# A transformer-like block on one core: P7's weights from the kept T2, P2 in P7's stage, late LayerNorm 2 vectors

## The chip, the cores and the metric

The kernel runs on one core of one Trainium2 chip. The metric is the device time of one execution in microseconds, the median over several runs. A second number is the span of the one execution that was profiled: from its first to its last instruction on the chip.

## What is computed

One layer on 512 tokens of width 2048, in float32 with float32 accuracy:

```python
h = layer_norm(x, ln_in_g, ln_in_b)
u = h @ w_in                                   # pool values | q | k | v
m = concat(multi_scale_pool(pool values), stick_breaking_attention(q, k, v)) @ w_out
h = layer_norm(alpha * h + m, ln1_g, ln1_b)
f = relu(h @ w_ff1 + b_ff1) ** 2               # 512 x 8192
f = f @ w_ff2 + b_ff2                          # 8192 x 2048 weights, 64 MiB
out = layer_norm(alpha * h + f, ln2_g, ln2_b)
```

Only the last two lines are touched by the change.

## The kernel before, in words

Each float32 product is made of three passes of the reduced type: an operand is split into a high and a low part, and a helper (`three`, L280) adds high x high, high x low and low x high in one PSUM bank. A weight is loaded (`w2_unit`, L726: 256 rows x 512 columns, 512 KB), its high part is a copy by ScalarE (`th`, L737) and its low part a subtraction by VectorE (`tl`, L738); both by `parts` (L733).

The product with `w_ff2` is done by Winograd's form of Strassen's method, with seven products in place of eight. The inner dimension of 8192 is cut into 16 blocks of 512, four blocks (`PER`) to a slice, so there are four slices (`slice_of`, L757). In each block the left operand is a 2 x 2 of A11, A12, A22 and A21 (tokens in two halves, inner dimension in two halves of 256). Its seven combinations were made earlier and stored to DRAM by POOL (`fh_d`, `fl_d`, L699); `operand` (L716) loads one of them for a whole slice as two tiles of 1 MiB (`oh`, `ol`) on POOL's queue. Four operands have room at a time, so the one asked for fifth takes the buffers of the first. The right operand is a 2 x 2 of b11, b12, b21 and b22 (inner halves, column halves), worked on in columns of 512: n = 0, 1 is the left half, n + 2 the right half. A unit is one product for one (n, u), u being the block in the slice: 12 matmuls. The weights of the products follow a chain kept in SBUF, a tile `c` for each of the eight (n, u):

- stage 1: b11 (P1, operand A11) and T1 = b12 - b11 (P5, operand S1; `c`, L775);
- stage 2: T2 = b22 - T1 (P6, operand S2; `c`, L789) and b22 (P3, operand S4);
- stage 3: b22 - b12 (P7, operand S3; L804), with b22 and b12 loaded again (`b22b`, `b12b`);
- stage 4: b21 (P2, operand A12) and b21 - T2 (P4, operand A22; `c`, L817); in the last slice all of P2, then `norm_out` for token blocks 0 and 1, then P4 for n = 0, then for n = 1 by token blocks, with a `norm_out` after each.

`x` banks collect P1, P6, P7 and P4; `v` banks P5 and P3; `w` banks P2. VectorE adds them to the rows `acc` (L752) after each n.

What sets the order: each engine and each DMA queue works through its instructions in a fixed order. The framework lays that order out when the kernel is built, by priorities and a simulated time line; what stands under `with ahead()` has its priority raised by 400 instructions, so that weights are prepared ahead of the matmuls. How far ahead is bounded by buffers: six `raw` tiles for weights under way (three each in two pools, in turn), four pairs of `th` and `tl`. Weight loads go out on SP's queue, operands on POOL's. At the entry of the slices the `right` pool takes over memory that the stage before held.

`norm_out` (L848) is LayerNorm 2 of 128 tokens: `bn_stats` by VectorE, a short chain of small operations, two operations of 512 columns for each quarter of the row (L859 and L860, with the vectors `ln2g` and `ln2b`) and the store (L861, SP). The first `norm_out` in program order asks for the two vectors (L852, SP, 1 MiB each as spread over 128 partitions), which depend on nothing but the memory of their tiles.

Of the kernel before, what the change touches and what calls it, by code (L numbers as in the profile page):

```python
# [9 lines left out]
F32 = mybir.dt.float32  # L10
F32R = mybir.dt.float32r
AF = mybir.ActivationFunctionType
ALU = mybir.AluOpType

P = 128
N = 512
# [7 lines left out]
def block_kernel(  # L24
# [18 lines left out]
    nc = tc.nc  # L43
# [5 lines left out]
    NQ = D // N  # L49
# [38 lines left out]
    def after(ins, earlier):  # L88

        tc.add_manual_dep(ins.ins, earlier.ins.name, mybir.DependencyInfo(  # L90
            mybir.DependencyClass.Sync, mybir.DependencyReason.DATA), reason="whole bank")
# [188 lines left out]
    def three(bank, a, b, first, last, free=False):  # L280
        (ah, al), (bh, bl) = a, b
        for n, (l, r) in enumerate(((ah, bh), (ah, bl), (al, bh))):
            mm = nc.tensor.matmul(bank, l, r, start=first and n == 0, stop=last and n == 2, skip_group_check=free)  # L283
        return mm
# [246 lines left out]
    for half in range(2):  # L531
        if half:
            v_block(half)
        for pair in (2 * half, 2 * half + 1):
            parts = qk_block(pair)
# [37 lines left out]
    for q in range(NQ - 1):  # L573
        banks = product(cols(w_out2, q * N, order), order, mixh, mixl, [f"o{q}_{tb}" for tb in range(NT)], False,
                        beside_first if q == 0 else
                        lambda i, mm: normed(q, i // 2, i % 2, mm))
# [65 lines left out]
    for t0 in (0, 2 * P):  # L642
        ts_ = slice(t0, t0 + 2 * P)
# [7 lines left out]
    for q in range(NQ):  # L651
        gb = tmp.tile([P, N], F32, tag="w", bufs=3, name=f"g1_{q}")
# [15 lines left out]
    first = pool(ctx, "first", 2, side="right")  # L668
# [4 lines left out]
    PER = 4  # L673
# [34 lines left out]
    right = pool(late, "right", 2)  # L708
# [7 lines left out]
    def operand(s, o):  # L716

        pl = right if turn("op", 2) else first
        both = []
        for d, n in ((fh_d, "h"), (fl_d, "l")):  # L720
            t = pl.tile([P, PER, 2, H2], F32R, tag=f"o{n}", bufs=2, name=f"o{n}{s}_{o}")
            nc.gpsimd.dma_start(f(t), d[s][o].rearrange("p u (i t) -> p u i t", i=2))
            both.append(t)
        return both

    def w2_unit(b, half, q, name):  # L726

        k0 = b * N + half * H2
        raw = (right if turn("raw") else wp).tile([P, 2, N], F32, tag="raw", bufs=3, name=name)
        nc.sync.dma_start(raw, w2[k0:k0 + H2, q * N:(q + 1) * N].rearrange("(c p) n -> p c n", p=P))  # L730
        return raw

    def parts(t, name):  # L733
        pl = right if turn("parts") else wp
        h = pl.tile([P, 2, N], F32R, tag="wh", bufs=2, name=f"th_{name}")
        l = pl.tile([P, 2, N], F32R, tag="wl", bufs=2, name=f"tl_{name}")
        nc.scalar.copy(h, t)  # L737
        nc.vector.tensor_tensor(l, t, f(h), op=ALU.subtract)  # L738
        return h, l

    def times(banks, op, u, w, first, last, ts=(0, 1)):
        (ah, al), (wh, wl) = op, w
        for i in range(2):
            for t in ts:
                ts_ = slice(t * P, (t + 1) * P)
                three(banks[t], (ah[:, u, i, ts_], al[:, u, i, ts_]), (wh[:, i, :], wl[:, i, :]),
                      first and i == 0, last and i == 1, True)

    def accumulate(banks, tb0, q, ts=(0, 1)):
        for t in ts:  # L750
            a = acc[tb0 + t][q]
            nc.vector.tensor_tensor(a, a, banks[t], op=ALU.add)  # L752
# [4 lines left out]
    def slice_of(s):  # L757

        end = s == NS - 1
        ahead = lambda: tc.high_priority(offset=400)  # L760
        units = range(PER)
        x = [pair(f"x{s}_{n}", f"x{n}") for n in range(2)]
        v = [pair(f"v{s}_{n}", f"v{n}") for n in range(2)]
        chain = {}
        with ahead():
            A11, S1 = operand(s, 0), operand(s, 3)
        for n in range(2):
            for u in units:
                b, at, e = s * PER + u, f"{s}_{n}_{u}", (u == 0, u == PER - 1)
                with ahead():  # L770
                    b11 = w2_unit(b, 0, n, f"b11_{at}")
                    b12 = w2_unit(b, 0, n + 2, f"b12_{at}")
                    p1 = parts(b11, f"1_{at}")
                    c = chain[n, u] = right.tile([P, 2, N], F32, tag=f"c{n}{u}", bufs=1, name=f"c_{at}")
                    nc.vector.tensor_tensor(c, b12, b11, op=ALU.subtract)  # L775
                    p5 = parts(c, f"5_{at}")
                times(x[n], A11, u, p1, *e)
                times(v[n], S1, u, p5, *e)
            accumulate(x[n], 0, n)
            accumulate(v[n], 2, n + 2)  # L780
        with ahead():
            S2, S4 = operand(s, 4), operand(s, 6)
        for n in range(2):
            for u in units:
                b, at, e = s * PER + u, f"{s}_{n}_{u}", (False, u == PER - 1)
                with ahead():
                    b22 = w2_unit(b, 1, n + 2, f"b22_{at}")
                    c = chain[n, u]
                    nc.vector.tensor_tensor(c, b22, c, op=ALU.subtract)  # L789
                    p6 = parts(c, f"6_{at}")  # L790
                    p3 = parts(b22, f"3_{at}")
                times(x[n], S2, u, p6, *e)
                times(v[n], S4, u, p3, *e)
            accumulate(x[n], 0, n + 2)
            accumulate(v[n], 0, n + 2)
        with ahead():
            S3 = operand(s, 5)
        for n in range(2):
            for u in units:
                b, at, e = s * PER + u, f"{s}_{n}_{u}", (False, u == PER - 1)  # L800
                with ahead():
                    b22 = w2_unit(b, 1, n + 2, f"b22b_{at}")
                    b12 = w2_unit(b, 0, n + 2, f"b12b_{at}")
                    nc.vector.tensor_tensor(b22, b22, b12, op=ALU.subtract)  # L804
                    p7 = parts(b22, f"7_{at}")
                times(x[n], S3, u, p7, *e)
            accumulate(x[n], 2, n + 2)
        with ahead():
            A12, A22 = operand(s, 1), operand(s, 2)
        w = [pair(f"w{s}_{n}", f"v{n}") for n in range(2)]  # L810

        def second(n, u):
            at = f"{s}_{n}_{u}"
            with ahead():
                b21 = w2_unit(s * PER + u, 1, n, f"b21_{at}")
                c = chain[n, u]
                nc.vector.tensor_tensor(c, b21, c, op=ALU.subtract)  # L817
                p2 = parts(b21, f"2_{at}")
            times(w[n], A12, u, p2, u == 0, u == PER - 1)

        def fourth(n, u):
            with ahead():
                return parts(chain[n, u], f"4_{s}_{n}_{u}")

        for n in range(2):
            for u in units:
                second(n, u)
                if not end:
                    times(x[n], A22, u, fourth(n, u), False, u == PER - 1)
            accumulate(w[n], 0, n)  # L830
            if not end:
                accumulate(x[n], 2, n)
        if end:
            for tb in range(2):
                norm_out(tb)
            for u in units:
                times(x[0], A22, u, fourth(0, u), False, u == PER - 1)
            accumulate(x[0], 2, 0)
            p4 = [fourth(1, u) for u in units]
            for t in range(2):  # L840
                for u in units:
                    times(x[1], A22, u, p4[u], False, u == PER - 1, (t,))
                accumulate(x[1], 2, 1, (t,))
                norm_out(2 + t)

    gb = {}

    def norm_out(tb):  # L848
        if not gb:
            for n, vec in (("g", ln2_g[0]), ("b", ln2_b[0])):  # L850
                t = gb[n] = right.tile([P, NQ, N], F32, tag=f"ln2{n}", bufs=1, name=f"ln2{n}")
                nc.sync.dma_start(t, vec.rearrange("(q n) -> q n", n=N).partition_broadcast(P))  # L852
        st = small.tile([P, NQ, 6], F32, name=f"st2_{tb}", tag="st")
        for q in (2, 3, 0, 1):
            nc.vector.bn_stats(st[:, q, :], acc[tb][q])
        mu, rs = finish_stats(st, f"n2{tb}", const)
        for q in range(NQ):
            a = acc[tb][q]
            nc.vector.scalar_tensor_tensor(a, a, mu, gb["g"][:, q, :], op0=ALU.subtract, op1=ALU.mult)  # L859
            nc.vector.scalar_tensor_tensor(a, a, rs, gb["b"][:, q, :], op0=ALU.mult, op1=ALU.add)  # L860
            nc.sync.dma_start(out2[tb * P:(tb + 1) * P, q * N:(q + 1) * N], a)  # L861
# [36 lines left out]
```

## Time and profile before

| | us |
|---|---|
| median of 3 runs (lowest to highest) | 2025.33 (2020.68 to 2026.61) |
| the profiled execution | 2028.36 |
| its span | 2026.7 |
| TensorE busy (share of the span) | 1940.9 (96%) |
| VectorE busy | 1216.1 (60%) |
| ScalarE busy | 739.4 (36%) |

PE is TensorE, PEld its weight load, DVE VectorE, ACT ScalarE, POOL GpSimd, SP SyncE; L12 is line 12 of the kernel. Times in rows are from the start of the span. A busy PE is not a PE at its peak: matmuls are pipelined, so the number of matmuls in a stretch tells more than the busy time. A wait is put down to what came last by the profile.

### The profile page before, as it was taken

Reading aid. Unit: us, or ns where it says so; the run is one execution under the profiler, and the core shown is the slowest. Engines: PE = TensorE matmul, PEld = TensorE weight load, DVE = VectorE, ACT = ScalarE, POOL = GpSimd, SP = SyncE. Lnnn points to the kernel's source line nnn. Section 1 sums busy time; section 2 is a strip of 40 time slices with the busy share of each in tenths; the row PEclk is TensorE's granted clock in tenths of the full one; section 3 lists DMA queues with packets and bytes.
Section 4 is the critical chain, followed back from the end, with each engine's and each line's share of the span. In section 5 each row is a group of like instructions: output and inputs, shape, how many; then the busy total and the mean of one; then the engine's idle time right before and its main releaser. Section 6 shows DMA issues by size and latency. Waiting matters only on the chain.

```text
span 2026.7 us, 22165 instructions
## 1 busy us (share of the span) xinstructions
PE 1940.9 (96%) x8736; PEld 1595.6 (79%) x8736; DVE 1216.1 (60%) x1513; ACT 739.4 (36%) x898; POOL 115.4 (6%) x162
## 2 busy tenths in 40 slices
PE   6999999999999999999999999969999999999995
PEld 4888888878889888888888888847788778778774
DVE  8445565675469544444344444348677687577788
ACT  3344554651124233333333333324343243333331
POOL 5000000000000000110000010010000000000000
PEclk9999999999999999999999999989999999999998
DMA  5022222225344455755555565567767766587562
GB/s 219 32 93 74 83 84 83 84 89 194 105 137 136 140 166 168 263 206 195 175 166 166 175 206 200 174 252 279 266 224 259 260 212 243 206 295 256 191 224 83
DMA packets 155399, 358.03 MB, mean 177 GB/s; under 512 B 10144, under 2 KB 27680, under 8 KB 147488
## 3 DMA queue, kind: packets, MB, share of 16 engines
q1 hardware_dynamic: 131728, 239.11, 36.2%
q0 software_dynamic: 23424, 117.45, 15.1%
q8 instruction: 68, 1.11, 0.2%
q14 instruction: 35, 0.29, 0.0%
q10 hardware_dynamic: 144, 0.07, 0.0%
HBM read 293.67 MB, written 62.91 MB: 176 GB/s over the span
## 4 chain that ended last, share of the span: by engine, by line
PE 53%; issue 23%; DVE 10%; DMA 10%; POOL 2%; ACT 1%; SPq 0%; DVEq 0%; POOLq 0%; ACTq 0%
PE f L210 9%; PE qk L361 9%; PE x L283 6%; PE o L210 6%; DMA b<-in_w_ff_dram 5%; PE p L210 4%; PE v L283 4%; DVE tl L738 4%; DMA b22b<-in_w_ff_dram 4%; PE o L283 3%; PE w L283 3%; PE f L283 2%; PE v L210 2%; POOL fh_d L699 1%; POOL fl_d L699 1%
## 5 line engine op out<-in xcount | busy, mean ns | idle before, releaser
L210 PE MATMUL f<-h1l,wh_f 128*128 128x512 f32 x960 | 373.8, 389 | 0.0
L210 PE MATMUL f<-h1h,wh_f 128*128 128x512 f32 x960 | 373.8, 389 | 0.0
L210 PE MATMUL f<-h1h,wl_f 128*128 128x512 f32 x960 | 347.1, 389 | 0.0
L184 DVE TENSOR_TENSOR wl_f<-raw_f,wh_f 128x1024 fp32r<-128x1024 f32 x120 | 146.8, 1224 | 276.3 <-ACT wh_f L183 276.3
L183 ACT CAST wh_f<-raw_f 128x1024 fp32r<-128x1024 f32 x120 | 126.4, 1053 | 361.4 <-PE f L210 320.9
L283 PE MATMUL x<-th,oh 128*128 128x512 f32 x512 | 195.8, 397 | 21.2 <-ACT th L737 21.0
L210 PEld LDWEIGHTS f<-h1h,wl_f 128*128 128x128 f32 x960 | 180.3, 188 | 37.4
L210 PEld LDWEIGHTS f<-h1l,wh_f 128*128 128x128 f32 x960 | 180.2, 188 | 37.3
L210 PEld LDWEIGHTS f<-h1h,wh_f 128*128 128x128 f32 x960 | 180.2, 188 | 37.3
L283 PE MATMUL x<-tl,oh 128*128 128x512 f32 x512 | 203.9, 398 | 5.2 <-DVE tl L738 4.8
L283 PE MATMUL x<-th,ol 128*128 128x512 f32 x512 | 202.0, 394 | 0.0
L737 ACT CAST th<-b 128x1024 fp32r<-128x1024 f32 x96 | 100.9, 1052 | 178.9 <-PE v L283 64.6
L737 ACT CAST th<-c 128x1024 fp32r<-128x1024 f32 x96 | 101.1, 1053 | 155.3 <-PE x L283 97.1
L738 DVE TENSOR_TENSOR tl<-b,th 128x1024 fp32r<-128x1024 f32 x96 | 117.0, 1220 | 36.4 <-ACT th L737 36.4
L283 PEld LDWEIGHTS x<-th,oh 128*128 128x128 f32 x512 | 96.1, 189 | 46.4 <-ACT th L737 24.3
L738 DVE TENSOR_TENSOR tl<-c,th 128x1024 fp32r<-128x1024 f32 x96 | 116.9, 1220 | 21.0 <-ACT th L737 20.8
L283 PEld LDWEIGHTS x<-tl,oh 128*128 128x128 f32 x512 | 96.9, 189 | 33.3 <-DVE tl L738 12.0
L283 PEld LDWEIGHTS x<-th,ol 128*128 128x128 f32 x512 | 96.9, 189 | 21.3
L283 PE MATMUL v<-th,oh 128*128 128x512 f32 x256 | 98.9, 398 | 10.5 <-ACT th L737 10.5
L283 PE MATMUL v<-tl,oh 128*128 128x512 f32 x256 | 102.3, 400 | 6.9 <-DVE tl L738 6.9
L283 PE MATMUL v<-th,ol 128*128 128x512 f32 x256 | 101.7, 397 | 0.0
L697 DVE TENSOR_TENSOR fl<-g,fh 128x1792 fp32r<-128x1792 f32 x32 | 64.8, 2025 | 61.4 <-DMA fl_d<-fl 53.8
(212 smaller groups left out, 3453.8 us busy)
## 6 DMA issues: line engine op xcount, KB each, us to landing
b<-in_w_ff_dram SPq DMA_DIRECT2D x128, 512.0 KB, 5.0
raw_f<-in_w_ff_dram SPq DMA_DIRECT2D x120, 512.0 KB, 3.9
fh_d<-fh POOLq DMA_DIRECT2D x32, 896.0 KB, 5.3
fl_d<-fl POOLq DMA_DIRECT2D x32, 896.0 KB, 5.9
oh<-fh_d POOLq DMA_DIRECT2D x28, 1024.0 KB, 7.9
ol<-fl_d POOLq DMA_DIRECT2D x28, 1024.0 KB, 10.6
raw_qk<-in_w_in_dram SPq DMA_DIRECT2D x64, 256.0 KB, 2.9
b22b<-in_w_ff_dram SPq DMA_DIRECT2D x32, 512.0 KB, 6.3
```

The costliest lines, as they stand in the source:

```text
L183: nc.scalar.copy(h, raw)
L184: nc.vector.tensor_tensor(l, raw, f(h), op=ALU.subtract)
L210: mm = nc.tensor.matmul(bank, a, b, start=first and n == 0, stop=last and n == 2)
L283: mm = nc.tensor.matmul(bank, l, r, start=first and n == 0, stop=last and n == 2, skip_group_check=free)
L361: nc.tensor.matmul(bank, a, b, start=kc == 0 and n == 0, stop=kc == KC - 1 and n == 2)
L697: nc.vector.tensor_tensor(l, full, f(h), op=ALU.subtract)
L699: nc.gpsimd.dma_start(d[b // PER][:, :, b % PER, i * H2:(i + 1) * H2].rearrange("o p t -> p o t"), f(t))
L737: nc.scalar.copy(h, t)
L738: nc.vector.tensor_tensor(l, t, f(h), op=ALU.subtract)
```

## The change

In slices 0 to 2, P7's weight b22 - b12 is made as T2 - b11, from the kept `c` and one load of b11. P7 and P2 then alternate in one stage, and `c` becomes b21 - T2 right behind P2's unit; P4 follows as a stage of its own without loads. A22 is asked for after that shared stage in program order. In the last slice P2 comes first, then `norm_out` for token blocks 0 and 1, then P7 (with the same new weight), then P4, for which b21 is loaded a second time, since `c` must stay T2 until P7 is made. The LayerNorm 2 vectors are loaded on POOL's queue, after the last matmul of the last slice's stage 2.

```diff
@@ times
-                three(banks[t], ...)
+                mm = three(banks[t], ...)
+        return mm
@@ slice_of, stage 2
-                times(v[n], S4, u, p3, *e)
+                mm = times(v[n], S4, u, p3, *e)
@@ slice_of, stages 3 and 4
         with ahead():
-            S3 = operand(s, 5)
-        for n in range(2):
-            for u in units:
-                with ahead():
-                    b22 = w2_unit(b, 1, n + 2, f"b22b_{at}")
-                    b12 = w2_unit(b, 0, n + 2, f"b12b_{at}")
-                    nc.vector.tensor_tensor(b22, b22, b12, op=ALU.subtract)
-                    p7 = parts(b22, f"7_{at}")
-                times(x[n], S3, u, p7, *e)
-            accumulate(x[n], 2, n + 2)
-        with ahead():
-            A12, A22 = operand(s, 1), operand(s, 2)
+            S3, A12 = operand(s, 5), operand(s, 1)
         w = [pair(f"w{s}_{n}", f"v{n}") for n in range(2)]
+        def third(n, u):
+            with ahead():
+                b11 = w2_unit(s * PER + u, 0, n, f"b11b_{at}")
+                nc.vector.tensor_tensor(b11, chain[n, u], b11, op=ALU.subtract)
+                p7 = parts(b11, f"7_{at}")
+            times(x[n], S3, u, p7, False, u == PER - 1)
         def second(n, u):
             with ahead():
                 b21 = w2_unit(s * PER + u, 1, n, ...)
-                c = chain[n, u]
-                nc.vector.tensor_tensor(c, b21, c, op=ALU.subtract)
                 p2 = parts(b21, ...)
             times(w[n], A12, u, p2, u == 0, u == PER - 1)
+            return b21
+        def last_of(n, u, b21):
+            with ahead():
+                c = chain[n, u]
+                nc.vector.tensor_tensor(c, b21, c, op=ALU.subtract)
...
+        if not end:
+            for n in range(2):
+                for u in units:
+                    third(n, u)
+                    last_of(n, u, second(n, u))
+                accumulate(x[n], 2, n + 2)
+                accumulate(w[n], 0, n)
+            with ahead():
+                A22 = operand(s, 2)
+            for n in range(2):
+                for u in units:
+                    times(x[n], A22, u, fourth(n, u), False, u == PER - 1)
+                accumulate(x[n], 2, n)
+            return
+        load_vectors(mm)
         for n in range(2):
             for u in units:
                 second(n, u)
-                if not end:
-                    times(x[n], A22, u, fourth(n, u), False, u == PER - 1)
             accumulate(w[n], 0, n)
...
+        with ahead():
+            A22 = operand(s, 2)
+        for tb in range(2):
+            norm_out(tb)
+        for n in range(2):
+            for u in units:
+                third(n, u)
+            accumulate(x[n], 2, n + 2)
+        for u in units:
+            with ahead():
+                last_of(0, u, w2_unit(s * PER + u, 1, 0, f"b21b_{s}_0_{u}"))
+            times(x[0], A22, u, fourth(0, u), False, u == PER - 1)
+        accumulate(x[0], 2, 0)
...
+    def load_vectors(mm):
+        for n, vec in (("g", ln2_g[0]), ("b", ln2_b[0])):
+            t = gb[n] = right.tile([P, NQ, N], F32, tag=f"ln2{n}", bufs=1, name=f"ln2{n}")
+            after(nc.gpsimd.dma_start(t, vec.rearrange("(q n) -> q n", n=N).partition_broadcast(P)), mm)
     def norm_out(tb):
-        if not gb:
-            for n, vec in (("g", ln2_g[0]), ("b", ln2_b[0])):
-                t = gb[n] = right.tile([P, NQ, N], F32, tag=f"ln2{n}", bufs=1, name=f"ln2{n}")
-                nc.sync.dma_start(t, vec.rearrange("(q n) -> q n", n=N).partition_broadcast(P))
```

P4 for n = 1 in the last slice loads b21 again in the same way and runs by token blocks, with a `norm_out` after each, as before.

## Rows read from the trace of the kernel before

**Rows 1.** The page: part 1, then DMA issues (count, KB each, us to landing).

```profile
PE 1940.9 (96%) x8736; PEld 1595.6 (79%) x8736; DVE 1216.1 (60%) x1513; ACT 739.4 (36%) x898; POOL 115.4 (6%) x162
...
b<-in_w_ff_dram SPq DMA_DIRECT2D x128, 512.0 KB, 5.0
...
oh<-fh_d POOLq DMA_DIRECT2D x28, 1024.0 KB, 7.9
```

**Rows 2.** Stretches: length, busy time (instructions) per engine, PE clock, DMA share, GB/s.

```profile
1525.00:1550.00 25.00, 25.00 (x110) 20.35 (x110) 21.00 (x21) 9.49 (x9) 0.00 (x0) 1.00 0.70 248
...
1350.00:1375.00 25.00, 14.53 (x48) 10.81 (x48) 8.18 (x8) 4.40 (x5) 0.00 (x0) 0.74 1.01 394
...
1370.00:1375.00 5.00, 4.96 (x14) 3.48 (x15) 4.83 (x5) 2.30 (x3) 0.00 (x0) 0.65 1.05 406
...
2000.00:2025.00 25.00, 6.00 (x27) 4.63 (x25) 22.80 (x48) 0.48 (x2) 0.00 (x0) 0.67 0.47 168
```

**Rows 3.** Timeline of PE: start, us, instruction, idle before it and its releaser.

```profile
1348.41 1.22 PE L283 MATMUL v<-th,oh 128*128 128x512 f32 x2 [10.46 <-ACT th L737]
...
1369.78 1.22 PE L283 MATMUL x<-th,oh 128*128 128x512 f32 x2 [10.43 <-ACT th L737]
...
1453.53 0.49 PE L283 MATMUL x<-th,oh 128*128 128x512 f32 x1 [1.16 <-ACT th L737]
...
1735.43 0.80 PE L283 MATMUL v<-tl,oh 128*128 128x512 f32 x1 [4.72 <-DVE tl L738]
```

**Rows 4.** Stretches of P7, tile x: length, busy (PE, PEld, DVE), clock, DMA.

```profile
1443.56:1473.00 29.44, 24.97 (x98) 18.64 (x96) 2.06 (x3) 0.94 0.93 345
1605.22:1633.86 28.64, 23.42 (x97) 17.64 (x96) 2.05 (x3) 1.00 0.92 346
1773.39:1801.21 27.82, 23.45 (x97) 17.66 (x96) 1.96 (x3) 1.00 0.94 353
```

**Rows 5.** Groups by line, 1376 to 2006 us: busy, mean ns, idle before.

```profile
L804 DVE TENSOR_TENSOR b22b<-b22b,b12b 128x1024 f32<-128x1024 f32 x32 | 38.8, 1223 | 45.4 <-DMA b22b<-in_w_ff_dram 31.1 <-issue 9.7 <-DMA b12b<-in_w_ff_dram 4.7
```

**Rows 6.** SP's waits, 1300 to 1360 us: total, times, longest.

```profile
SPq L852 <- DMA fh_d<-fh: 26.2, 1, 26.2
```

**Rows 7.** Timeline of SP's queue.

```profile
1348.31 0.34 SPq L852 DMA_DIRECT2D ln2g<-in_ln_g_dram  x1
...
2003.92 19.24 SPq L861 DMA_DIRECT2D out_dram<-acc  x16
```

**Rows 8.** The chain that ended last: start, us, what.

```profile
1352.14 16.52 DMA b<-in_w_ff_dram
...
1446.50 12.87 DMA b22b<-in_w_ff_dram
```

**Rows 9.** Timeline of VectorE.

```profile
1346.06 2.35 DVE L775 TENSOR_TENSOR c<-b,b 128x1024 f32<-128x1024 f32 x2
...
1733.02 1.22 DVE L789 TENSOR_TENSOR c<-b,c 128x1024 f32<-128x1024 f32 x1 [8.20 <-DMA b<-in_w_ff_dram]
...
2003.14 5.39 DVE L860 SCALAR_TENSOR_TENSOR acc<-acc,rs_n,ln2b 128x512 f32<-128x512 f32 x8
...
2017.42 5.38 DVE L860 SCALAR_TENSOR_TENSOR acc<-acc,rs_n,ln2b 128x512 f32<-128x512 f32 x8
```

**Rows 10.** Timeline of POOL: operand loads at the entry and in the last slice.

```profile
1347.38 0.58 POOL L722 DMA_DIRECT2D oh<-fh_d  x1
...
1935.00 0.53 POOL L722 DMA_DIRECT2D oh<-fh_d  x1 [44.15 <-issue]
```

**Rows 11.** Groups of VectorE by line, 1935 to 2027 us (columns as in rows 5).

```profile
L738 DVE TENSOR_TENSOR tl<-c,th 128x1024 fp32r<-128x1024 f32 x8 | 9.7, 1215 | 1.6 <-ACT th L737 1.5
L817 DVE TENSOR_TENSOR c<-b,c 128x1024 f32<-128x1024 f32 x8 | 9.7, 1220 | 0.5 <-DMA b<-in_w_ff_dram 0.5
...
L738 DVE TENSOR_TENSOR tl<-b22b,th 128x1024 fp32r<-128x1024 f32 x6 | 7.3, 1217 | 0.0
L804 DVE TENSOR_TENSOR b22b<-b22b,b12b 128x1024 f32<-128x1024 f32 x5 | 6.0, 1221 | 5.2 <-issue 4.1 <-DMA b22b<-in_w_ff_dram 1.1
```

More of the change, by code (lines that the diff above doesn't have):

```diff
@@ L745, in times @@
                 ts_ = slice(t * P, (t + 1) * P)
-                three(banks[t], (ah[:, u, i, ts_], al[:, u, i, ts_]), (wh[:, i, :], wl[:, i, :]),
-                      first and i == 0, last and i == 1, True)
+                mm = three(banks[t], (ah[:, u, i, ts_], al[:, u, i, ts_]), (wh[:, i, :], wl[:, i, :]),
+                           first and i == 0, last and i == 1, True)
+        return mm
     def accumulate(banks, tb0, q, ts=(0, 1)):
@@ L796, in slice_of, with second @@
         with ahead():
-            S3 = operand(s, 5)
-        for n in range(2):
-            for u in units:
-                b, at, e = s * PER + u, f"{s}_{n}_{u}", (False, u == PER - 1)
-                with ahead():
-                    b22 = w2_unit(b, 1, n + 2, f"b22b_{at}")
-                    b12 = w2_unit(b, 0, n + 2, f"b12b_{at}")
-                    nc.vector.tensor_tensor(b22, b22, b12, op=ALU.subtract)
-                    p7 = parts(b22, f"7_{at}")
-                times(x[n], S3, u, p7, *e)
-            accumulate(x[n], 2, n + 2)
-        with ahead():
-            A12, A22 = operand(s, 1), operand(s, 2)
+            S3, A12 = operand(s, 5), operand(s, 1)
         w = [pair(f"w{s}_{n}", f"v{n}") for n in range(2)]
-        def second(n, u):
+        def third(n, u):
             at = f"{s}_{n}_{u}"
             with ahead():
-                b21 = w2_unit(s * PER + u, 1, n, f"b21_{at}")
+                b11 = w2_unit(s * PER + u, 0, n, f"b11b_{at}")
+                nc.vector.tensor_tensor(b11, chain[n, u], b11, op=ALU.subtract)
+                p7 = parts(b11, f"7_{at}")
+            times(x[n], S3, u, p7, False, u == PER - 1)
+        def second(n, u):
+            with ahead():
+                b21 = w2_unit(s * PER + u, 1, n, f"b21_{s}_{n}_{u}")
+                p2 = parts(b21, f"2_{s}_{n}_{u}")
+            times(w[n], A12, u, p2, u == 0, u == PER - 1)
+            return b21
+        def last_of(n, u, b21):
+            with ahead():
                 c = chain[n, u]
                 nc.vector.tensor_tensor(c, b21, c, op=ALU.subtract)
-                p2 = parts(b21, f"2_{at}")
-            times(w[n], A12, u, p2, u == 0, u == PER - 1)
         def fourth(n, u):
@@ L827, in slice_of @@
                 second(n, u)
-                if not end:
-                    times(x[n], A22, u, fourth(n, u), False, u == PER - 1)
             accumulate(w[n], 0, n)
[L831 to L835, printed above, removed]
-            for u in units:
[L837 to L844, printed above, removed]
+        with ahead():
[3 more added lines that the diff above has]
+        for n in range(2):
+            for u in units:
+                third(n, u)
[5 more added lines that the diff above has]
+        accumulate(x[0], 2, 0)
+        p4 = []
+        for u in units:
+            with ahead():
+                last_of(1, u, w2_unit(s * PER + u, 1, 1, f"b21b_{s}_1_{u}"))
+            p4.append(fourth(1, u))
+        for t in range(2):
+            for u in units:
+                times(x[1], A22, u, p4[u], False, u == PER - 1, (t,))
+            accumulate(x[1], 2, 1, (t,))
+            norm_out(2 + t)
     gb = {}
+    def load_vectors(mm):
+        for n, vec in (("g", ln2_g[0]), ("b", ln2_b[0])):
+            t = gb[n] = right.tile([P, NQ, N], F32, tag=f"ln2{n}", bufs=1, name=f"ln2{n}")
+            after(nc.gpsimd.dma_start(t, vec.rearrange("(q n) -> q n", n=N).partition_broadcast(P)), mm)
     def norm_out(tb):
-        if not gb:
-            for n, vec in (("g", ln2_g[0]), ("b", ln2_b[0])):
-                t = gb[n] = right.tile([P, NQ, N], F32, tag=f"ln2{n}", bufs=1, name=f"ln2{n}")
-                nc.sync.dma_start(t, vec.rearrange("(q n) -> q n", n=N).partition_broadcast(P))
         st = small.tile([P, NQ, 6], F32, name=f"st2_{tb}", tag="st")
```

## The prediction

> **What bounds the kernel now.** I read the views in this order: the page's busy shares, the stretches of 25 us, PE's waits, the timelines of PE, SP, POOL and VectorE around each gap, and the last 90 us by line. TensorE is busy 96% of the span [rows 1]. The change touches only the slice part, from 1329 us on, and that part runs differently. Undisturbed it makes 110 matmuls in 25 us [rows 2], 0.2273 us each, so one unit of 12 matmuls takes 2.73 us, and a stage of one product (8 units) 21.8 us. Time is lost there in four places:
>
> - the entry: two gaps of 10.46 and 10.43 us [rows 3];
> - the P7 stage of each slice, where 96 matmuls took 29.44, 28.64 and 27.82 us in the first three slices, with the DMA engines 92 to 94% busy [rows 4]; that is 7.6 + 6.8 + 6.0 = 20.4 us above 21.8 each. A gap there ends on a weight's cast [rows 3], the cast waits for the subtraction of L804, and that for a load: 31.1 + 4.7 us of idle before 32 of them [rows 5];
> - the start of stage 2 in the third slice, a gap of 4.72 us [rows 3];
> - the tail: of the 25 us from 2000 us PE is busy for 6.00, VectorE for 22.80 [rows 2]; the span ends at 2026.7.
>
> **The entry (A).** SP had put six loads into the six `raw` buffers and then stood 26.2 us [rows 6] in front of `ln2g`, whose memory a store of `fh` still held. The two vectors (1 MiB each) went out from 1348.31 on [rows 7]; the seventh weight load, at 1352.14, landed 16.52 us later [rows 8], and with it the second gap ended. The change takes the vectors off SP. The first gap stays: it waits for `c` of L775 at 1346.06 [rows 9], which comes behind the last block's `fl` on VectorE, and neither is touched. The seventh load needs the buffer that the first `c` frees, so it can go at about 1347.3, 4.9 us sooner; and 2.10 MB less lie ahead of it, 5.3 us at the 394 GB/s of that stretch [rows 2]. It would land near 1358.5, about when PE runs out (1369.78 - 10.43 = 1359.35). With some 2.4 us for cast and subtraction, a gap of 1.5 to 2 remains. The gap's aftermath shrinks too: at a mean clock of 0.65 PE ran 14 matmuls in the 5 us from 1370 [rows 2], where 22 fit. I take -9. Ends: -12.4 (the whole gap and 2 us of low clock), and -3, if the operand tiles issued from 1347.38 on [rows 10] hold the eighth load back as long as the seventh was held (1347.6 + 16.5 = 1364.1, and 2.4 to PE).
>
> **P7 and P2 in one stage (B, slices 0 to 2).** Removed: one 512 KB load per unit (b22b and b12b become b11b), 24 in three slices. VectorE's count stays: one subtraction and one `tl` for P7, one `tl` and one `c` for P2. Moved: P7's 8 units and P2's 8 now alternate over 43.7 us with 16 loads, where P7 alone asked for 16 in 21.8 us. The operand tiles that the end of stage 2 frees (4 of 1 MiB, 4.2 MB) still come there in a burst. Bytes: 16 x 0.524 + 4.2 = 12.6 MB in 43.7 us, 288 GB/s, where P7 was to take them in 21.8 and ran at 345 to 353 GB/s [rows 4]. A weight load caught in the burst took 12.87 us [rows 8] against 5.0 in the median [rows 1]. Before, P7's first gap came 10 us into the stage (1453.53 [rows 3] against 1443.56 [rows 4]), so about four units, eight loads, were ready; eight loads are now eight units of 2.73 us, 22 us of cover. Against it: VectorE needs four operations per pair of units, 1.13 us each (two of L775 in 2.35, one of L789 in 1.22), and eight `acc` per stage, 0.67 each as L860 (eight in 5.39) [rows 9]: 36.2 + 5.4 = 41.6 us of 43.7, and its order is fixed. At a stage 2 boundary one `c` that waited 8.20 us for a load at VectorE's head [rows 9] cost PE the 4.72 us gap, with one load per two units only. Something like that can stay: I leave 2.7 us per slice. B = -20.4 + 8 = -12.4; ends -20.4 and 0 (each boundary paying some 7 us, as P7 does now). The fourth product alone needs no load: 8 casts and 8 `tl` in 21.8 us, while the next slice's first six loads come in. I cost it at nothing; without that cover its tiles would come in a burst at the entry of the next stage 1, as they did, where PE shows no gap.
>
> POOL's queue: S3, A12 and A22 are asked for in the same sequence, so each takes the buffer it took before. S3's buffer is given back a stage later, as the next slice's S1 needs it 22 us after that; a tile takes 7.9 us [rows 1]. That I cost at nothing; without those 22 us stage 1 would begin a tile's 7.9 us late.
>
> **The last slice (D).** Here P2 runs first, then P7, then P4, with b21 loaded again: three loads per unit, as before (b22b, b12b, b21). The vectors wait on POOL for stage 2's last matmul. Queued beside them is only A22, which is needed 44 us later: two vectors and its two tiles, 4.2 MB, the size of the other bursts. VectorE is what counts. From 1935.00, where A22's load went out at the end of stage 2 [rows 10], to 2022.80, the end of its last operation [rows 9], are 87.8 us, of which it was idle 5.2 + 1.6 + 0.5 = 7.3 [rows 11]. The work of the three stages and the four `norm_out` is the same afterwards, except for what is done ahead: of P7's 8 subtractions and 8 `tl` only 5 and 6 fall into that window [rows 11], so 5 were done; afterwards it is about three `tl` of P2, so 2 operations, 2.3 us, more remain. New idle: P2's stage asks for only 8 `tl` (9.0 us of 21.8); P7's subtractions fill it only as their loads come through the burst. Bounds: all idle gone, 2.3 - 7.3 = -5; P2's stage filled with nothing but its own `tl`, two `acc` and four `bn_stats` (9.0 + 6 x 0.67 = 13.0), +8.8 of idle and 2.3 of work, +11. The block of 5.39 us before the last accumulations [rows 9] breaks up, but that is order, not work. I take +3. SP now has eight stores between its loads; before, all 16 came after the last load, from 2003.92 [rows 7].
>
> The 4.72 us at a stage 2 boundary I leave; such gaps may move by a few us either way.
>
> **Sum.** -9 - 12.4 + 3 = -18.4. The profiled execution took 2028.36 us (span 2026.7 and 1.66 around it): 2010.0. It lies 3.0 above the median 2025.33, so 2007.
>
> **The page's rule.** The b22b load of 12.87 us went out on SP at 1446.50 [rows 8], while POOL's tiles of that boundary were moving. The Trainium skill, "DMA: Bandwidth & Descriptors", section "Issuing engines are not separate DMA queues", says that transfers started by SP, ACT or POOL run on the same 16 engines and interleave, so another issuer saves only issue time. By that the vectors' 2.1 MB are moved, not hidden: they land in the burst at P2's start. By that rule alone P2's start pays (rival 3); the 12.87 us agree with it.
>
> **Rivals.**
>
> 1. *VectorE paces the shared stage.* For: 41 of 43.7 us, and the 8.20 us wait that cost PE 4.72. Against: all 35.8 us before L804 [rows 5] are waits for loads, of which half go. Then B is 0: -9 + 3 = -6, 2019.
> 2. *The entry's loads starve all the same.* For: four tiles go out from 1347.38 on, with the new issue time [rows 10]. A is -3: -12.4, 2013.
> 3. *The vectors starve P2's start.* P2's units would come as P7's did at its boundary, some 7 us late: D = +10, -11.4, 2014. Against: P2 needs one load per unit, and six are in before the burst.
> 4. *Slower: stores and `norm_out` in front of the last loads.* If VectorE does `norm_out` of rows 0 and 1 (16 operations of 0.67 us and the small ones, 12 us) before P7's weights, and SP's eight stores wait for it with P4's b21b loads behind them, PE stands for 12 us and then for a load of 12.9, plus a few us at low clock: some 28 us, D = +28: -21.4 + 28 = +6.6, 2032. It decides from 21.4 us on. For: SP did stand 26.2 us before one transfer [rows 6] with PE paying. Against: the weights' instructions are put 400 places ahead, and six buffers lie between.
>
> **Chances.** Forecast 0.54, rival 1 0.14, rival 2 0.12, rival 3 0.09, rival 4 0.11. About 0.3% (6 us) can be told from no change, so faster is below 2019.3: forecast (less 0.02), rivals 2 and 3 make 0.73 and a share of rival 1 0.01, so 0.74; the rest of rival 1 and of the forecast, 0.15, is the same; rival 4, 0.11, slower. The forecast's own range is 1996 to 2015 (A, B and D seldom at one end together); with rival 1 it reaches 2021, which leaves out rival 4 and the extremes.
>
> **What would show it.** After: no vector near 1348, the load after the sixth near 1347, a second gap under 4 us; P7 and P2 together near 46 us per slice with DMA near 70%; P4 near 22; VectorE idle below 10 us from the end of stage 2 to its end. Wrong would be: a second entry gap of 8 us, shared stages of 50 us, or PE gaps in the last 66 us that end on b21b, with SP waiting at its stores.

## The result: 1.0% slower

The changed kernel takes 2046.45 us in the median of four runs (2045.58 to 2047.2), the kernel before 2025.97 beside it: a ratio of 1.0104 [1.0081, 1.0126]. Its profiled execution took 2046.89 us, with a span of 2045.2. The prediction said 2007 and a chance of 0.11 for slower. It was wrong by 39 us, and in sign.

Part 1 of the page, its DMA total and one DMA issue:

```profile
PE 1950.1 (95%) x8736; PEld 1603.7 (78%) x8736; DVE 1216.8 (59%) x1513; ACT 739.9 (36%) x898; POOL 116.5 (6%) x164
...
DMA packets 148871, 345.44 MB, mean 169 GB/s; under 512 B 9760, under 2 KB 27296, under 8 KB 140960
...
b<-in_w_ff_dram SPq DMA_DIRECT2D x128, 512.0 KB, 4.4
```

PE's count of matmuls is that of [rows 1], and DMA moves 12.6 MB less than before (358.03 MB): the 24 loads are gone. So the work did shrink, and the time went into waiting.

Where it went is read from POOL's timeline: an operand tile is asked for when a stage's last matmul releases its buffer, so consecutive issues give each stage's length. At the end of slice 3's stage 2 POOL issues something only after the change (`ln2g` at 1954.10, 0.69 us after the start of the last matmul on `v`). Before, that matmul starts at 1935.99, so the end is put at 1936.68. Before and after, in us, from the two traces:

| stretch | before | after | difference |
|---|---|---|---|
| to the end of stage 2 of slice 0 | 1443.56 | 1437.25 | -6.3 |
| slice 0: P7, P2, P4 | 73.3 | 72.9 | -0.4 |
| slice 1: stages 1 and 2 | 88.4 | 99.3 | +10.9 |
| slice 1: P7, P2, P4 | 73.4 | 72.1 | -1.3 |
| slice 2: stages 1 and 2 | 94.8 | 100.8 | +6.0 |
| slice 2: P7, P2, P4 | 72.2 | 72.5 | +0.3 |
| slice 3: stages 1 and 2 | 91.1 | 99.2 | +8.1 |
| last slice from there | 90.0 | 91.1 | +1.1 |

They sum to +18.4; the spans differ by 18.5. More than all of it, +25.0, is in stages 1 and 2 of slices 1 to 3, whose products, loads and tiles are what they were: 17.1 in the three stages 2 and 7.9 in the three stages 1. The shared stage is no gain: with P4 it takes what the two old stages took.

By stretches, columns as in [rows 2]: slice 1's stage 1, stage 2, shared stage and P4 stage of the changed kernel.

```profile
1510.12:1557.13 47.01, 45.16 (x193) 35.63 (x191) 31.63 (x32) 16.89 (x17) 2.15 (x5) 1.00 0.55 188
1557.13:1609.50 52.37, 46.19 (x194) 37.21 (x194) 36.13 (x37) 16.83 (x17) 2.10 (x5) 0.93 0.48 170
1609.50:1659.20 49.70, 46.06 (x194) 37.08 (x193) 37.08 (x37) 16.80 (x17) 2.07 (x5) 0.97 0.72 252
1659.20:1681.60 22.40, 22.40 (x98) 18.04 (x97) 15.08 (x16) 8.40 (x9) 1.05 (x3) 1.00 0.65 247
```

The same 193 matmuls need 47.01, 52.37 and 49.70 us where 43.7 is the undisturbed length. In the longest DMA is at 0.48 and VectorE busy for 36.13 of 52.37: neither is full. So something waits. PE's timeline, the entry's second gap and then stage 2 and the shared stage of slices 1 and 2 (columns as in [rows 3]):

```profile
1366.28 0.74 PE L283 MATMUL x<-th,oh 128*128 128x512 f32 x2 [4.44 <-ACT th L737]
...
1571.97 0.79 PE L283 MATMUL v<-tl,oh 128*128 128x512 f32 x1 [6.18 <-DVE tl L738]
1621.95 0.50 PE L283 MATMUL w<-tl,oh 128*128 128x512 f32 x1 [3.63 <-DVE tl L738]
...
1743.16 0.79 PE L283 MATMUL v<-tl,oh 128*128 128x512 f32 x1 [6.33 <-DVE tl L738]
1794.82 0.80 PE L283 MATMUL w<-tl,oh 128*128 128x512 f32 x1 [3.66 <-DVE tl L738]
```

The entry's gap fell from 10.43 [rows 3] to 4.44. In slices 1 to 3 stage 2 now has a gap of 5.1 to 6.3 us (v) in its first half, where before slice 2 had one of 4.72 [rows 3] and slice 3 one of 2.18; each of the three shared stages has one of 3.5 to 3.7 (w). All of these (not the entry's) end on a low part `tl`, that is on VectorE. The gap is not the whole loss: slice 1's stage 2 is 8.2 us longer than before (52.37 against 44.16), of which its gap is 6.18, and in the 4 us behind the gap, at a mean granted clock of 0.60 (mostly the lower of its two levels), PE made 11 matmuls where 17 to 18 fit undisturbed. VectorE's timeline up to the gap at 1571.97:

```profile
1557.10 1.22 DVE L738 TENSOR_TENSOR tl<-b,th 128x1024 fp32r<-128x1024 f32 x1
1558.23 1.28 DVE L753 TENSOR_TENSOR acc<-acc,x 128x512 f32<-128x512 f32 x2
1559.43 1.22 DVE L738 TENSOR_TENSOR tl<-c,th 128x1024 fp32r<-128x1024 f32 x1
1560.56 0.68 DVE L753 TENSOR_TENSOR acc<-acc,v 128x512 f32<-128x512 f32 x1
1568.96 1.23 DVE L790 TENSOR_TENSOR c<-b,c 128x1024 f32<-128x1024 f32 x1 [7.72 <-DMA b<-in_w_ff_dram]
1570.10 0.68 DVE L753 TENSOR_TENSOR acc<-acc,v 128x512 f32<-128x512 f32 x1
1570.70 1.22 DVE L738 TENSOR_TENSOR tl<-b,th 128x1024 fp32r<-128x1024 f32 x1
1571.84 1.22 DVE L738 TENSOR_TENSOR tl<-c,th 128x1024 fp32r<-128x1024 f32 x1
1572.97 1.22 DVE L738 TENSOR_TENSOR tl<-b,th 128x1024 fp32r<-128x1024 f32 x1
1574.11 1.22 DVE L738 TENSOR_TENSOR tl<-c,th 128x1024 fp32r<-128x1024 f32 x1
```

A subtraction `c` stands at the head of VectorE for 7.72 us and waits for a load. Behind it are an accumulation and four `tl` that then run back to back, none with a wait of its own; PE's next matmul starts 1.27 us after the first of them. The chain of waits of this stretch names the loop:

```profile
1554.82 1.22 DVE c L790
1556.04 2.28 DVE tl L738 x2
1558.32 0.02 issue
1558.34 10.60 DMA b<-in_w_ff_dram
1568.94 0.02 issue
1568.96 1.23 DVE c L790
1570.19 0.60 DVE acc L753
1570.78 1.15 DVE tl L738
1571.93 0.04 issue
1571.97 4.25 PE v L283 x11
```

The load goes out the moment a `tl` is done and a raw buffer is free; it takes 10.60 us where the median is 4.4, among the four operand tiles of the stage's end, which go out from 1554.28 on; and the `c` that wants it blocks the `tl` that PE wants. Before the change the same race was nearly even. In slice 1 load and first tile went out at 1558.27 and 1558.26, `c` waited 0.93 us, and there was no gap; in slice 3 at 1887.66 and 1887.04, with a gap of 2.18; in slice 2 at 1721.32 and 1719.43, which is the 8.20 us wait of [rows 9] and the gap of 4.72. After, the load is 4 to 5 us behind the tiles in all three slices (1558.34 and 1554.28; 1729.27 and 1725.18; 1903.62 and 1898.82). Why the change puts it that far behind was not traced.

In the shared stages it is another subtraction that stands there: `c` = b21 - T2 (L819), which the change moved into them, right behind P2's unit. It waits for b21's load for 7.44, 7.22 and 7.42 us in slices 0 to 2, just before the gaps of 3.49, 3.63 and 3.66. In slice 1:

```profile
1618.94 1.22 DVE L819 TENSOR_TENSOR c<-b,c 128x1024 f32<-128x1024 f32 x1 [7.22 <-DMA b<-in_w_ff_dram]
```

VectorE's waits from 1370 to 1954 us (total, times, longest):

```profile
DVE tl L738 <- ACT th L737: 67.3, 59, 2.8
DVE c L790 <- DMA b<-in_w_ff_dram: 37.1, 18, 8.0
DVE c L776 <- DMA b<-in_w_ff_dram: 34.6, 10, 8.1
DVE c L819 <- DMA b<-in_w_ff_dram: 27.9, 7, 7.4
DVE b11b L805 <- DMA b11b<-in_w_ff_dram: 3.5, 5, 1.1
```

Before, from 1370 to 1937 us (L775 is stage 1's `c`, L789 stage 2's, L817 b21's):

```profile
DVE c L775 <- DMA b<-in_w_ff_dram: 36.2, 15, 4.4
DVE c L789 <- DMA b<-in_w_ff_dram: 20.1, 9, 8.2
DVE c L817 <- DMA b<-in_w_ff_dram: 2.3, 3, 1.1
```

After the change that makes 103 us of waits for loads, single ones of up to 8 us, and P7's new subtraction (L805) has only 3.5 of them. Before it was 93 us, with 34.7 for P7's old one (L804). The waits moved from P7's weights [rows 5] to the subtractions of stage 2 (L790) and of b21 (L819); stage 1's (L776) are as they were.

### The profile page after: what moved, and what is told of

It is laid out like the page before. It is cut to its first block, busy times and chain, and to the rows that moved or that the text cites. A ratio compares the mean times of both kernels' runs of the same rounds, so it can differ in the third digit from the quotient of the medians.

```text
span 2045.2 us, 22127 instructions
## 1 busy us (share of the span) xinstructions
PE 1950.1 (95%) x8736; PEld 1603.7 (78%) x8736; DVE 1216.8 (59%) x1513; ACT 739.9 (36%) x898; POOL 116.5 (6%) x164
## 4 chain that ended last, share of the span: by engine, by line
PE 54%; issue 22%; DMA 11%; DVE 10%; POOL 2%; ACT 1%; SPq 0%; DVEq 0%; POOLq 0%; ACTq 0%
DMA b<-in_w_ff_dram 9%; PE f L210 9%; PE qk L361 9%; PE x L283 7%; PE o L210 6%; PE p L210 4%; PE v L283 4%; DVE tl L738 4%; PE w L283 3%; PE o L283 3%; PE f L283 2%; PE v L210 2%; DMA b11b<-in_w_ff_dram 1%; POOL fh_d L699 1%; POOL fl_d L699 1%
## 5 line engine op out<-in xcount | busy, mean ns | idle before, releaser
L738 DVE TENSOR_TENSOR tl<-b,th 128x1024 fp32r<-128x1024 f32 x96 | 117.0, 1219 | 44.8 <-ACT th L737 44.8
```

## The experiments

Two theories at the start. **H:** loads land late at the boundaries because the operand tiles are moving; in its *burst* form the length of the burst decides, in its *order* form that VectorE's fixed order puts a `c` with a fresh load ahead of `tl` whose data are there. **V** (rival 1): VectorE's 41.6 us of work paces the shared stage.

### 1. Half the operand tiles (e1)

The low tile is left out and the high one used in its place; PE, VectorE and ScalarE have the same instructions to work through.

```diff
-        for d, n in ((fh_d, "h"), (fl_d, "l")):
...
-        return both
+        t = pl.tile([P, PER, 2, H2], F32R, tag="oh", bufs=2, name=f"oh{s}_{o}")
+        nc.gpsimd.dma_start(f(t), fh_d[s][o].rearrange("p u (i t) -> p u i t", i=2))
+        return [t, t]
```

> The changed kernel, but each operand comes as one tile of 1 MiB in place of two (the low part is left out and the high tile used in its place), so the bursts at the stage boundaries are half as long and all instructions on PE, VectorE and ScalarE stay. Theory H (a weight load that goes out inside such a burst lands 10 to 14 us later, and the subtraction that needs it stands at VectorE's head): the gaps at the starts of stages 1, 2 and 3 fall below 2 us each, 2046 becomes 2000 to 2015. Rival V (VectorE's 41 of 43.7 us pace the shared stage): that stage stays near 50 us, the total above 2030.

2029.49 us, ratio 1.0012 [0.9994, 1.0031]: 17 us below the changed kernel, and less of a gain than the burst form expected. Slice 1's stage 1, stage 2 and shared stage, by stretches:

```profile
1502.75:1552.42 49.67, 45.46 (x192) 35.20 (x190) 31.35 (x30) 16.82 (x17) 1.06 (x3) 1.00 0.47 156
1552.42:1598.33 45.91, 44.78 (x194) 36.23 (x195) 31.63 (x32) 16.84 (x17) 1.05 (x2) 1.00 0.36 128
1598.33:1650.93 52.60, 47.93 (x193) 38.15 (x192) 41.91 (x42) 16.83 (x17) 1.06 (x2) 0.94 0.64 218
```

Stage 2 gets 6.5 us back, the other two get longer. The load at the end of slice 1's stage 1 takes 5.40 us now, where it took 10.60 among twice as many tiles, and the entry's second gap is gone. So the burst makes the loads late. But the next wait opens (a gap of 6.45 us in slice 2's shared stage): a shorter burst moves the stops; it doesn't end them. This run does not exclude V: its shared stages take 49 to 53 us.

### 2. VectorE's order: each subtraction behind the fourth-last low part (e2)

`after` makes an instruction wait for an earlier one, here a subtraction for the `tl` that was made four before it in the program. At most three of the low parts made before it can then come behind it.

```diff
-        nc.vector.tensor_tensor(l, t, f(h), op=ALU.subtract)
+        tls.append(nc.vector.tensor_tensor(l, t, f(h), op=ALU.subtract))
...
+    tls = []
+    def behind(ins):
+        if len(tls) >= 4:
+            after(ins, tls[-4])
...
-  nc.vector.tensor_tensor(c, b22, c, op=ALU.subtract)
+  behind(nc.vector.tensor_tensor(c, b22, c, op=ALU.subtract))
```

The last two lines stand for all four subtractions of the slices (L776, L790, L805, L819). Work, loads and tiles are unchanged.

> The changed kernel, but each subtraction that needs a fresh load is ordered on VectorE behind the low part made four before it, so that it can no longer stand in front of low parts whose data are there. Bursts and bytes stay. Theory H in its order form: the 6.2, 6.3 and 5.1 us gaps at the start of stage 2 shrink to under 2 us, and the total falls by 15 to 30, to 2016 to 2031. If the bytes alone are the cause (the loads are late whatever the order): within 5 of 2046. Rival V: within 5 of 2046.

1997.93 us (1997.68 to 1997.95), ratio 0.9851 [0.9816, 0.9886]: 48 us less than the changed kernel, more than expected. The same three stages, and the last slice from the end of stage 2:

```profile
1504.39:1548.55 44.16, 44.16 (x193) 36.00 (x192) 33.80 (x33) 16.87 (x17) 2.10 (x5) 1.00 0.61 210
1548.55:1592.71 44.16, 44.16 (x194) 36.02 (x193) 35.41 (x35) 16.85 (x17) 2.09 (x5) 1.00 0.54 199
1592.71:1636.93 44.22, 44.22 (x193) 36.00 (x192) 36.34 (x36) 16.74 (x17) 2.10 (x5) 1.00 0.76 275
...
1902.10:1996.20 94.10, 69.57 (x287) 54.06 (x285) 82.18 (x120) 22.83 (x25) 1.05 (x2) 0.91 0.50 178
```

PE is busy for the whole of each stage, the shared one too (44.22), with VectorE at 36.34 us in it: V falls. (36 of its operations fall in, not the 40 of the sum of 41.6 us.) VectorE's waits for loads fell from 103 to 21 us (to 1954, so its first part of the last slice is in):

```profile
DVE tl L738 <- ACT th L737: 96.6, 113, 2.5
DVE b11b L811 <- DMA b11b<-in_w_ff_dram: 10.2, 4, 4.0
DVE c L825 <- DMA b<-in_w_ff_dram: 7.8, 3, 3.4
DVE c L782 <- DMA b<-in_w_ff_dram: 2.8, 2, 1.9
```

The rule does two things, which no run separates. At the starts of stage 2 the load is on time again: in slice 1 it goes out at 1545.33, the first tile at 1545.75, and it lands in 4.3 us (4.2 in slices 2 and 3). In the shared stages the loads are as late as ever and PE runs on: four that go out between 1590 and 1599 us, at the start of slice 1's, by their medians:

```profile
b<-in_w_ff_dram SPq DMA_DIRECT2D x2, 512.0 KB, 11.3
b11b<-in_w_ff_dram SPq DMA_DIRECT2D x2, 512.0 KB, 13.1
```

There a late load does no harm, as long as the `tl` that PE wants don't stand behind its subtraction.

### 3. The same rule with ten (e9)

```diff
-        if len(tls) >= 4:
-            after(ins, tls[-4])
+        if len(tls) >= 10:
+            after(ins, tls[-10])
```

> The changed kernel with the order rule at ten low parts in place of four: a subtraction may stand that much further ahead. Theory H in its order form: the nearer to the old order, the more of the gaps come back; 2015 to 2040. If it is not the order but some side effect of the rule (such as another order on the other queues): as with four, within 5 of 1998.

2050.36 us, ratio 1.0109 [1.0081, 1.0137]: the changed kernel again, with gaps at the stage 2 boundaries of 5.88, 6.68 and 6.18 us. So it isn't the extra dependency that helps but how far ahead a subtraction may stand. A limit of ten changes next to nothing, which suggests that the planned order puts subtractions more than four and seldom more than ten low parts ahead; the order itself was not listed.

### 4. The rule in the kernel before (e5)

The edit of e2, in before.

> The kernel before with only the order rule of the second experiment (each subtraction that needs a fresh load stands behind the low part made four before it). Theory H: the 4.7 and 2.2 us gaps at stage 2 go, the P7 stages keep theirs, since there 16 loads and the tiles must come in 21.8 us whatever the order: 2026 becomes 2010 to 2018. If the change's stages are no better than the old ones once the order is mended (rival: the whole gain of the second experiment is the order's): about 2000, as there.

2021.7 us, ratio 0.9973 [0.996, 0.9987]. The gap at stage 2 of slice 2 goes; P7's stages stay at 29.4, 29.75 and 28.45 us, with gaps of 3.91, 4.33 and 4.11. So the order alone does not mend P7's lateness; e6 and e7 below show that it takes the rule together with one load per unit in place of two.

### 5. Late vectors alone (e3), one load alone (e4), both (e7), both with the rule (e6)

All in the kernel before, with its four stages and its last slice:

```diff
 # e3, e7, e6: the vectors from POOL after stage 2's last matmul
-                nc.sync.dma_start(t, vec.rearrange(...))
+            after(nc.gpsimd.dma_start(t, vec.rearrange(...)), mm)
 # e4, e7, e6: P7's weight from the kept T2 and one load
-                    b22 = w2_unit(b, 1, n + 2, f"b22b_{at}")
-                    b12 = w2_unit(b, 0, n + 2, f"b12b_{at}")
-                    nc.vector.tensor_tensor(b22, b22, b12, op=ALU.subtract)
+                    b11 = w2_unit(b, 0, n, f"b11b_{at}")
+                    nc.vector.tensor_tensor(b11, chain[n, u], b11, op=ALU.subtract)
```

> The kernel before with nothing but the two LayerNorm vectors moved to POOL behind the last matmul of the last slice's stage 2. Term A of the prediction alone: 6 to 9 us faster than before, 2017 to 2020, the second entry gap under 5 us. If the entry's loads starve behind the operand tiles anyway: within 3 of before. If an earlier start of the slices worsens the later boundaries (a matter of timing, as in H): no gain or slower, with gaps of 4 to 6 us at the starts of stage 2.

2023.01 us, ratio 0.9976 [0.9958, 0.9994]. The second entry gap falls to 4.73, but from the end of stage 2 of the last slice on it takes 94.7 us instead of 90.0: there a P7 gap of 5.26 us appears, in the vectors' burst. Rival 3 asked whether that start pays; with P7 there it does.

> The kernel before with nothing but P7's weight made as T2 - b11 from one load, in its old stage of its own; P2 and P4 stay together. If P7's loads were what its stage waited for: its 27.8 to 29.4 us fall to 23 to 25, the total by 10 to 16, to 2010 to 2016. Theory H adds that the gap stays where a load still meets the burst: a fall of only 5 to 10. If the stage is paced by VectorE: no change.

2021.17 us, ratio 0.9969 [0.9949, 0.999]. P7's stages are 28.8, 24.2 and 23.2 us, about 10 less in all, and the stage 2 boundaries give half of it back: gaps of 3.32, 4.91 and 3.40, 11.6 in all, where before had 4.72 and 2.18. This is the change's loss in small, with the old stages: a saving in one stage turns into the same wait in another.

> The kernel before with one load for P7 and the late vectors, without the order rule. Apart they gave 4.9 and 3.0 us. If they add: 2016 to 2020. If the order rule is what lets them gain (with it the same kernel took 1990): 2016 or more, and gaps of 3 to 5 us at the starts of stage 2. If the two together are enough: 1990 to 2005.

2016.14 us, ratio 0.9924 [0.9897, 0.9951]; stage 2 gaps of 4.55 and 3.62, P7 gaps of 3.44, 3.52 and 2.24. The two edits together are not enough without the rule.

> The kernel before with the order rule, one load for P7 and the late vectors, but the old stages and the old last slice. Tells whether sharing a stage is worth anything. Theory H: P7's 8 loads, 4.2 MB in 21.8 us beside 4.2 MB of tiles, 385 GB/s, still leave a gap or two of 1 to 2 us per slice: 2002 to 2008. Rival (one load is all that was needed): 1996 to 2000, as the second experiment.

1990.33 us (1989.54 to 1991.42), ratio 0.9816 [0.9784, 0.9848]. After the entry PE has no gap over 1 us up to its last matmul. Its P7 stages in slices 0 and 1:

```profile
1437.61:1460.01 22.40, 22.40 (x97) 18.00 (x96) 18.59 (x19) 8.42 (x8) 1.05 (x2) 1.00 0.93 354
...
1592.50:1614.26 21.76, 21.76 (x97) 18.02 (x96) 18.27 (x19) 8.44 (x8) 1.05 (x2) 1.00 0.95 362
```

This is P7's stage of [rows 4] with the same DMA share, 0.93 to 0.95, at 354 and 362 GB/s (345 to 353 there), and PE doesn't stop once. A full DMA is no sufficient reason for P7's loss: with one load per unit and a `tl` that nothing holds up, the same share is harmless.

### 6. The rule without the new last slice (e10)

```diff
 # e2 with the old sequence in the last slice: P7, P2 (and T2's last step), norm_out of rows 0 and 1, P4
```

> The second experiment with the last slice in its old sequence (P7, then P2 with the subtraction, norm_out for blocks 0 and 1, then P4; b21 loaded once). Term D alone. If P2 first costs what the prediction gave it (+3): 1993 to 1997. If it gains, since norm_out of blocks 0 and 1 comes off the end: 2000 to 2006. If VectorE's total work alone sets the end: within 2 of 1998.

1990.09 us, ratio 0.9812 [0.9785, 0.9839]. Against e2 that is 7.8 us less. The last slice from the end of stage 2:

```profile
1902.85:1988.80 85.95, 65.63 (x287) 53.47 (x285) 76.44 (x116) 22.77 (x25) 1.04 (x2) 0.91 0.40 147
```

85.95 us against 94.10 for e2 with P2 first. Of the 8.15, VectorE's busy time makes 5.74 (76.44 against 82.18: four operations more remain, and the mean ones are a little longer) and its idle time 2.41. And e10 is level with e6, which has the old stages: the shared stage itself is worth nothing.

### 7. The rule in a part of the stages (e11, e12)

```diff
 # e11: behind(...) around L776 and L790 (stages 1 and 2) only
 # e12: behind(...) around L805 and L819 (shared stage) only
```

> The changed kernel with the order rule for the subtractions of stages 1 and 2 alone. In slices 1 to 3 those two stages were some 12 us per slice over 2 x 43.7, 37 us in all, the shared stages 6 to 7 each, 25 in all. If each stage's loss is made by its own subtractions: 2008 to 2014, with the shared stages still near 50. If the shared stage's late subtractions also make stages 1 and 2 late: 2020 to 2030. If one rule mends both: 1998.

2002.11 us, ratio 0.9859 [0.9822, 0.9897]. Only slice 0's shared stage stays long (51.4 us, a gap of 4.23); those of slices 1 and 2 are 44.9 and 43.5 without a rule of their own.

> The changed kernel with the order rule for the shared stage's subtractions (P7's weight and the new c) alone. If each stage's loss is its own: 2021 to 2027, stage 2 still near 52 in slices 1 to 3 and the shared stage 44 to 45. If the shared stage is what makes the next slice late: 2000 to 2010.

2035.76 us, ratio 1.0026 [1.001, 1.0042]. The shared stages are 44.8, 44.2 and 43.5 us, the stage 2 gaps stay, and so do the waits of `c` in stages 1 and 2:

```profile
DVE c L782 <- DMA b<-in_w_ff_dram: 36.0, 10, 8.7
DVE c L796 <- DMA b<-in_w_ff_dram: 35.8, 16, 7.9
```

In ratios to before the whole rule takes 1.0104 to 0.9851, 0.0253; stages 1 and 2 alone take 0.0245 (to 0.9859), the shared stage alone 0.0078 (to 1.0026). Each part mends where it stands. In slices 1 and 2, once stages 1 and 2 run through, the shared stage behind them is on time as well; in slice 0 it is not, though PE has no gap between the entry and its start there.

## Why the prediction was wrong, step by step

- **What bounds the kernel:** the places of loss were read rightly, but the reading stopped at "a load is late". The line that decided stood in it: a `c` of 8.20 us at VectorE's head, and a fixed order [rows 9].
- **A, the entry, -9:** right in mechanism. No vector goes out near 1348, the loads run on from 1346.53, and the second gap fell by 6.0 us to 4.44; up to the end of slice 0's stage 2 it gave 6.3. The remaining gap was to be 1.5 to 2. The load that it waited for was neither the seventh nor the eighth, which the prediction followed, but the ninth, out at 1347.66 beside the tiles that go out from 1346.57 on (in the chain of waits: `1347.66 17.50 DMA b<-in_w_ff_dram`). That is the hold of 16.5 us of the prediction's lower end, one load further on. With half the tiles (e1) the gap is gone.
- **B, the shared stage, -12.4:** failed. In the changed kernel it gave about -1.3, its own end of the range ("each boundary paying some 7 us, as P7 does now"). The residual of 2.7 us per slice was taken on the ground that eight loads are 22 us of cover. Cover in loads is no cover while VectorE may not make the next `tl`. The new `c` (L819) was counted as 1.13 us of work per pair of units; what it cost was a wait of over 7 us for its load, at VectorE's head, at the start of each shared stage.
- **"The 4.72 us at a stage 2 boundary I leave; such gaps may move by a few us either way":** this is the step that made the sign. It was costed at nothing; with the stages 1 of slices 1 to 3, which were taken as undisturbed, it cost 25.0 us (17.1 and 7.9). Without it the rows of the table come to -6.6. The wait had the same cause as B's residual, it stood in the trace where the load had missed the tiles by 1.9 us, and the boundaries were treated as noise instead of asking how close the other slices were to it (0.01 us in slice 1, 0.6 in slice 3).
- **D, the last slice, +3:** +1.1 in the changed kernel, with as much VectorE work as before (81.76 us against 81.51). Under the rule the new sequence costs 8.2 us (e2 against e10), within the bounds of -5 to +11; there the work was mis-sized: 5.7 us more of it remain, not 2.3.
- **The sum:** with the rule in both kernels the change brings 1997.93 against 2021.7, -24 us, which is near the predicted -18.4. There the late vectors and the saved load together are 31 us (e6 against e5). By the two traces, whose spans differ by 32.6, 5.2 of it come before the end of slice 0's stage 2 (A, taken at 9), 21.7 in the P7 stages of slices 0 to 2 (B, taken at 12.4 with 20.4 as its end) and 5.6 in the last slice, whose P7 has the saved load too, which the sum left out; D is +8. That the total comes near -18.4 is therefore in part luck: its terms miss in both directions. What the sum lacked was the fixed order that met them.
- **Rivals:** 1 (VectorE paces the stage) named the right place and the wrong mechanism: its stage did last 50 us, but from waits, not from work. 2 was in part real: 4.44 us of the entry's gap stayed. 3 was real for P7 (in e3 the loads of its start took some 12 us, before 6 to 7) and not seen for P2, whose stage begins without a gap. 4, the only slower one, did not occur: SP's stores all went out from 2022.72 on, after its last load, and held nothing up. The slower case that did occur was not among the rivals.

What stays open: why the planned order puts the subtractions so far ahead was not tried, nor why the change sets the loads 4 to 5 us behind the tiles. e2, e10 and e6 show that a limit of four mends it and e9 that ten doesn't; values between were not run. How much of the rule's gain is from loads that go out sooner, and how much from late loads that hold nothing up, is not known.

## What to carry to other kernels

When an in-order engine stands idle at an instruction that waits for a load, look at what runs back to back behind it: if those are the ones the bottleneck waits for, mend their order before you save bytes. Without that a saving can turn into the next wait (e1, e4); with it the saved load and the late vectors were worth 31 us. A gap that differs among equal places is a race; read by how much each wins or loses it before calling it noise, since a change of timing can lose all of them. Here one ordering rule was worth 48 us in the changed kernel and 4 in the old one (by the ratios 22 in the old one with late vectors and one load, e7 and e6), so edits should be judged with it in place: the best versions, late vectors and one load for P7 with the rule, take 1990 us, 1.8% less than before.

## What the runs showed of the hardware

A 512 KB weight load issued while four 1 MiB operand tiles were moving took 10.60 us, 4.4 in the median of the run; with two tiles in place of four, the load at the same place took 5.40 (e1). At the entry one took 17.50. DMA engines 93 to 95% busy at 354 to 362 GB/s are no sign of a DMA bound by themselves: in [rows 4] such a stage lost 6 to 7.6 us, in e6 the same share went with a PE that never stopped in the stage.
